# Order of the VectorE and ScalarE work between norm and up projection in a hybrid decoder layer

## The chip, the cores and the metric

The kernel runs on one core of a Trainium2 chip. The metric is the device time of one execution in microseconds; the kernel before took 1312.49 us (median of 3 runs, 1310.65 to 1314.9).

A core has engines that each work through a queue of their own in order: TensorE (PE in the profile) multiplies matrices, VectorE (DVE) does elementwise arithmetic on two operands, ScalarE (ACT) does copies and functions of one operand, GpSimd (POOL) does further elementwise work, and SyncE (SP) issues the DMAs here. [...] An instruction that waits holds up all that stands behind it on its engine.

## The reference, cut to what matters

One decoder layer on `x` of 1024 tokens by 1024 channels: a norm, one input projection whose columns feed differential attention and a gated delta rule, an output projection onto the residual, and a squared-ReLU MLP. The change lies at the start of that MLP.

```python
x = x + mix @ w_out[l]
h = rms_norm(x, norm2_w[l])
x = x + jnp.square(jax.nn.relu(h @ w_up[l])) @ w_down[l]
```

`h` is 1024 x 1024, `w_up` 1024 x 4096 and `w_down` 4096 x 1024, all in float32.

## The kernel before

Three things shape the part around the change.

First, each float32 matrix product is made of three matmuls on rounded operands: an operand is split into a rounded part (ACT: `S.copy`, L1124) and the rest, the operand minus its rounded part (DVE, L1125); the rest-by-rest product is left out. `split` does both, ACT first and then DVE.

Second, the up projection takes seven block products where plain 2 x 2 blocking takes eight (Strassen's way in Winograd's order). For that, sums and differences of blocks are made. On the side of `h` they are made once, for four tiles of 128 tokens (tb 0 to 3, the second block of tokens): `s1`, `s2` are the transposed halves of the tile's normed rows, `t1` and `t4` its differences to the tile four further on, kept in `kept`. The results are the operands hH/hL (rounded part and rest of `h`) and T_ops: T0 for product 6, T1 for product 7, T2 for product 4. On the side of `w_up` they are made for each of the eight groups g of 512 columns: four raw blocks a, b, c, d, of which `combine` makes the operands of the products 5, 6, 3 and 7 in place (`WS`, L1283: 5 is c = c + d, 6 is c = c - a, 3 is b = b - c, 7 is c = d - c), each of which is then split. An `op` tile is a rounded part or a rest; there are five.

Third, PE's order is written out by hand throughout. A product is 24 matmuls of 128 x 512. For group 0 the products 1 and 2 (into banks X0 and Y) run before the seam, as do those of group 1 (X1 and Z); then come, for group 0, product 5 (into Y, after `read_first` has read it), 6 (onto X0), 3 (onto Y), 7 (onto X0), then product 5 of group 1 (into Y afresh), and product 4 of group 0. Before a product is added onto a bank, the bank's value so far has to be copied out: Y to `d` by ACT (L1373), X to `c` by ACT (L1375), Y's sum into `c` by DVE (L1377).

The *seam* runs from L1264 to L1426. In it the order of DVE and of ACT is by hand too (`manual_schedule` over PE, DVE and ACT): the instructions of the seam stay in the order in which the program gives them, though work from before and behind it can be put between them. Outside the seam a planner orders DVE, ACT and the DMAs, by a model of the times of its own.

The steps that the seam orders are, for the four tiles, the stages of `held_back` (L1154), called by `held(stage, tiles)`: stage 0 is `second` (s1 from s2 and s1, L1150; split of the second half into hH/hL, L1151; s2 minus t1, L1152), stage 1 the split of T0, stage 2 the difference `t4` (L1154), stage 3 the split of T1, stage 4 the split of T2. For the operands they are `rounded(g, i)` (the combination, then ACT's rounding, L1326) and `rest(g, i)` (DVE's rest, L1330). `read_first` (L1239) copies X0 on ACT, adds Y on DVE, applies ReLU and square on ACT and stores the result. `step(g, i)` emits a product and what reads its bank. `load_w` (L1287) loads raw blocks for the coming groups, each into a buffer that must have come free.

The part of the seam that is not inside a function:

```python
held(0, [0, 1]); held(1, [0, 1]); rounded(0, 5); held(0, [2]); read_first(); rest(0, 5)
held(0, [3]); held(1, [2, 3]); rounded(0, 6); rest(0, 6)
...
rounded(0, 3); rest(0, 3); step(0, 5); held(3); held(2, [0, 1]); held(4, [0, 1])
rounded(0, 7); rest(0, 7); step(0, 6); held(2, [2, 3]); held(4, [2, 3])
for g, i in ((1, 1), (1, 2), (0, 3)): step(g, i)
```

(Printed with several calls on a line; in the program each has its own, L1336 to L1345 and L1413 to L1425.)

Of the kernel before, what the change touches and what calls it, by code (L numbers as in the profile page):

```python
# [9 lines left out]
F32 = mybir.dt.float32  # L10
# [3 lines left out]
ALU = mybir.AluOpType  # L14
# [90 lines left out]
def act(n, accum=False):  # L105
    return "S", 55.0 + 0.83 * n + (93.0 if accum else 0.0)


def vec(n, extra=0.0):
    return "V", 68.0 + 1.045 * n + extra  # L110
# [7 lines left out]
def tile_hymba_layer(  # L118
# [7 lines left out]
    V, S, G, T = nc.vector, nc.scalar, nc.gpsimd, nc.tensor  # L126
# [26 lines left out]
    hH = hpool.tile([P, KB, SEQ], F32R, name="hH")  # L153
    hL = hpool.tile([P, KB, SEQ], F32R, name="hL")
# [236 lines left out]
    def ta(name, bufs, dt=F32):  # L391
        return sa.tile([P, 512], dt, tag=name, name=name, bufs=bufs)
# [93 lines left out]
    for h, hf, y, th in skew(dn_proj(1)):  # L486
        k2 = ta("k2", 2)
# [5 lines left out]
        for c in range(4):  # L493
            i = cidx(h, 4 * hf + c)
# [9 lines left out]
        for c in range(4):  # L504
            i = cidx(h, 4 * hf + c)
# [56 lines left out]
    for h, hf, y, th in skew(dn_proj(0)):  # L562
        k2 = ta("kr", 2)
# [7 lines left out]
        for c in range(4):  # L571
            i = cidx(h, 4 * hf + c)
# [3 lines left out]
        for c in range(4):  # L576
            i = cidx(h, 4 * hf + c)
# [541 lines left out]
    normed_by, normed_at, held_back, banks, normed2, raws, kept, u, ups = [], {}, [], {}, set(), [], {}, {}, {}  # L1119
    k1, k2, tok1, tok2 = slice(0, 4), slice(4, 8), slice(512, 1024), slice(0, 512)  # L1120

    def split(dst, src):

        S.copy(dst[0], src)  # L1124
        V.tensor_tensor(dst[1], src, dst[0].bitcast(F32), ALU.subtract)  # L1125
# [5 lines left out]
    def turn_b(hn, t, tb):  # L1131
        sl = slice(tb * P, (tb + 1) * P)
        for i in range(2):
            r = yield from flow.bank("px", at=t)
            p = px.tile([P, 512], F32, tag="px", name="ps_tr")
            for j in range(4):
                T.transpose(p[:, j * P:(j + 1) * P], hn[i][:, j * P:(j + 1) * P], ident)
            S.copy(hn[i], p)
            flow.pe(4 * TR)
            t = flow.chain(act(512))  # L1140
            flow.hold(r, t)
        s1, s2 = [x.rearrange("p (k c) -> p k c", k=4) for x in hn]
        t1, t4 = kept[tb + 4][:, 0], kept[tb + 4][:, 1]
        T2, T3, T4 = [[x[:, :, sl] for x in o] for o in T_ops]
        V.tensor_tensor(t1, s1, t1, ALU.subtract)
        split((hH[:, k1, sl], hL[:, k1, sl]), t1)
        flow.chain(vec(512), act(512), vec(512), start=t)

        def second():
            V.tensor_tensor(s1, s2, s1, ALU.subtract)  # L1150
            split((hH[:, k2, sl], hL[:, k2, sl]), s2)  # L1151
            V.tensor_tensor(s2, s2, t1, ALU.subtract)  # L1152

        held_back.append((second, lambda: split(T2, s2), lambda: V.tensor_tensor(t4, t4, s2, ALU.subtract),  # L1154
                          lambda: split(T3, s1), lambda: split(T4, t4)))

    def backs():
        while len(normed_at) < NT:
            d = next((d for d in sorted(hns) if hns[d][1] <= flow.now), None)
            if d is None or not state["free"]:  # L1160
                yield flow.now + 50, None
                continue
            hn, t = hns.pop(d)
            if d < 4:
                keep(tiles[d])
                for i in range(2):
                    yield from turn(hn[i], t, tiles[d], 4 * i, kept[tiles[d]][:, i])
                feed()
                normed_at[d] = landed[tiles[d], 4]
            else:  # L1170
                yield from turn_b(hn, t, tiles[d])
                normed_at[d] = flow.now
# [66 lines left out]
    def read_first():  # L1239
        a0 = pools["uz"].tile([P, 2, 512], F32, tag="ua0", name="ua0")  # L1240
        S.copy(a0, banks["X0"])
        V.tensor_tensor(a0, a0, banks["Y"], ALU.add)
        act2(a0)
        nc.sync.dma_start(ud[1][0], a0)
        u[0] = {"a": a0}
# [66 lines left out]
    def flush(keep):  # L1312
        while len(puts) > keep:
            for d, t in puts.pop(0):
                nc.sync.dma_start(d, t)
# [3 lines left out]
    def combine(g, i):  # L1319
        dst, l, r, op = WS[i]  # L1320
        V.tensor_tensor(w[g][dst], w[g][l], w[g][r], op)

    def rounded(g, i):
        combine(g, i)
        early[g, i] = [op_.tile([P, 4, 256], F32R, tag="op", name="op", bufs=5) for _ in range(2)]
        S.copy(early[g, i][0], w[g][CH[i]])  # L1326

    def rest(g, i):
        o = early[g, i]
        V.tensor_tensor(o[1], w[g][CH[i]], o[0].bitcast(F32), ALU.subtract)  # L1330

    def held(stage, tbs=range(4)):
        for i in tbs:
            held_back[i][stage]()

    held(0, [0, 1])  # L1336
    held(1, [0, 1])
    rounded(0, 5)
    held(0, [2])
    read_first()  # L1340
    rest(0, 5)
    held(0, [3])
    held(1, [2, 3])
    rounded(0, 6)
    rest(0, 6)  # L1345

    def product(g, i):
        if i in WS and (g, i) not in early:
# [59 lines left out]
    def step(g, i):  # L1408
        puts.append([])
        product(g, i)  # L1410
        flush(2)

    rounded(0, 3)  # L1413
    rest(0, 3)
    step(0, 5)
    held(3)
    held(2, [0, 1])
    held(4, [0, 1])
    rounded(0, 7)
    rest(0, 7)  # L1420
    step(0, 6)
    held(2, [2, 3])
    held(4, [2, 3])
    for g, i in ((1, 1), (1, 2), (0, 3)):
        step(g, i)  # L1425
    seam.close()  # L1426
# [146 lines left out]
```

## Time and profile before

| | |
|---|---|
| median of 3 runs | 1312.49 us (1310.65 to 1314.9) |
| the profiled execution | 1312.03 us, its span 1310.2 us |
| PE busy | 1246.2 us (95% of the span) |
| DVE busy | 879.2 us (67%) |
| ACT busy | 599.3 us (46%) |
| POOL busy | 269.7 us (21%) |
| mean granted clock of TensorE | 0.986 |

The span is the time from the first to the last instruction of the profiled execution; 1.8 us of its time lie around it. Rows of a timeline give start, length, engine, source line, operation, the tile written and the tiles read, shapes, and how many like instructions are merged; in brackets stands the idle time of the engine before the row and what ended it. Lengths of neighbours on an engine overlap a little, so the time that a piece of work takes is the distance from its start to the next start. Where a helper makes an instruction, the row shows the helper's line: L1124 and L1125 are `split`, L1321 is `combine`.

### The profile page before, as it was taken

What the parts mean: (1) busy time and instruction counts of PE and PEld (TensorE: products, weight loads), DVE (VectorE), ACT (ScalarE), POOL (GpSimd) and SP (SyncE); (2) the same over time, 40 slices, a digit from 0 to 9 for tenths busy, and PEclk for the clock granted to TensorE, in tenths of its full rate; (3) what the DMA queues carried; (4) which work ended last, traced back from release to release, by engine and by line L of the source; (5) the groups of instructions that cost most, each with busy time, mean ns of one, the idle gap of its engine ahead of it and who ended that gap; (6) DMA issues with size and microseconds to landing.
All of it is one profiled execution on the core that took longest, in us unless ns stands there. A gap on an engine that the chain in (4) does not pass through costs nothing.

```text
span 1310.2 us, 18982 instructions
## 1 busy us (share of the span) xinstructions
PE 1246.2 (95%) x6925; PEld 1067.6 (81%) x6925; DVE 879.2 (67%) x1413; ACT 599.3 (46%) x1171; POOL 269.7 (21%) x320
## 2 busy tenths in 40 slices
PE   6998888999999899999999999999999999999998
PEld 6987666789898899788878788888887788888887
DVE  6469999856764876667478855555666775577552
ACT  5254433334343666555475645444554433333331
POOL 1048866124543542111220000000000000000000
PEclk9999889999998999999999999999999999999999
DMA  7144344436765464623343744334347955523311
GB/s 248 41 113 111 108 108 108 106 102 213 235 211 177 159 187 154 194 71 111 108 162 104 264 147 150 135 142 151 145 176 247 403 188 193 193 95 99 127 64 65
DMA packets 164775, 200.30 MB, mean 153 GB/s; under 512 B 20249, under 2 KB 125001, under 8 KB 164681
## 3 DMA queue, kind: packets, MB, share of 16 engines
q1 hardware_dynamic: 164680, 199.07, 46.4%
q8 instruction: 55, 0.90, 0.3%
q14 instruction: 40, 0.32, 0.1%
HBM read 132.97 MB, written 66.06 MB: 152 GB/s over the span
## 4 chain that ended last, share of the span: by engine, by line
PE 74%; DVE 14%; DMA 6%; issue 2%; ACT 2%; POOL 1%; SPq 1%; DVEq 0%; POOLq 0%; ACTq 0%
PE X L1202 4%; PE X L1203 4%; PE X L1204 4%; PE X L1495 4%; PE X L1494 4%; PE X L1496 4%; DVE cy L413 3%; PE ps_qk L790 3%; PE ps_qk L791 3%; PE ps_qk L792 3%; PE Y L1202 2%; PE Y L1203 2%; PE Y L1204 2%; PE ps_o L951 2%; PE ps_op L1038 2%
## 5 line engine op out<-in xcount | busy, mean ns | idle before, releaser
L1124 ACT CAST hH<-ur 128x1024 fp32r<-128x1024 f32 x56 | 58.6, 1050 | 175.1 <-PE Z L1495 83.7
L1125 DVE TENSOR_TENSOR hL<-ur,hH 128x1024 fp32r<-128x1024 f32 x56 | 68.3, 1222 | 83.5 <-ACT hH L1124 83.5
L790 PE MATMUL ps_qk<-wH,hH 128*128 128x256 f32 x384 | 114.9, 299 | 0.0
L791 PE MATMUL ps_qk<-wL,hH 128*128 128x256 f32 x384 | 109.0, 284 | 0.0
L792 PE MATMUL ps_qk<-wH,hL 128*128 128x256 f32 x384 | 109.0, 284 | 0.0
L1125 DVE TENSOR_TENSOR op<-raw,op 128x1024 fp32r<-128x1024 f32 x48 | 58.7, 1223 | 73.4 <-PE X L1203 38.7
L1495 PE MATMUL X<-hL,hH 128*128 128x512 f32 x224 | 87.3, 390 | 2.1 <-DVE hL L1125 2.1
L1494 PE MATMUL X<-hH 128*128 128x512 f32 x224 | 87.3, 390 | 1.6 <-DVE b L1393 1.6
L172 POOL TENSOR_TENSOR wL<-wraw,wH 128x512 fp32r<-128x512 f32 x56 | 72.8, 1311 | 70.5 <-ACT wH L171 70.2
L1496 PE MATMUL X<-hH,hL 128*128 128x512 f32 x224 | 87.2, 389 | 0.0
L177 PE MATMUL ps_dn<-hH,wH 128*128 128x512 f32 x192 | 77.8, 405 | 1.0 <-ACT cp L409 1.0
L178 PE MATMUL ps_dn<-hL,wH 128*128 128x512 f32 x192 | 77.9, 405 | 0.0
L179 PE MATMUL ps_dn<-hH,wL 128*128 128x512 f32 x192 | 77.1, 402 | 0.0
L790 PEld LDWEIGHTS ps_qk<-wH,hH 128*128 128x128 f32 x384 | 74.0, 193 | 0.1
L791 PEld LDWEIGHTS ps_qk<-wL,hH 128*128 128x128 f32 x384 | 73.6, 192 | 0.1
L792 PEld LDWEIGHTS ps_qk<-wH,hL 128*128 128x128 f32 x384 | 73.1, 190 | 0.0
L413 DVE SCALAR_TENSOR_TENSOR cy<-cp,pv,cy 128x512 f32<-128x512 f32 x72 | 65.7, 917 | 9.5 <-ACT cy L411 8.1
L1125 DVE TENSOR_TENSOR hL<-dw,hH 128x1024 fp32r<-128x1024 f32 x56 | 68.0, 1217 | 4.4 <-ACT hH L1124 4.4
L1124 ACT CAST op<-raw 128x1024 fp32r<-128x1024 f32 x48 | 50.4, 1052 | 34.5 <-PE Y L1204 19.9
L171 ACT CAST wH<-wraw 128x512 fp32r<-128x512 f32 (+1 forms) x72 | 42.9, 620 | 48.2 <-DMA wraw<-in_w_in_dram 36.4
L1124 ACT CAST hH<-dw 128x1024 fp32r<-128x1024 f32 x56 | 58.4, 1047 | 13.7 <-PE Z L1496 7.4
L912 ACT ACTIVATE pexp<-ps_sc,mx 128x128 f32<-128x128 f32 (+7 forms) x64 | 47.4, 742 | 26.6 <-DVE mx L908 26.1
(337 smaller groups left out, 3608.5 us busy)
## 6 DMA issues: line engine op xcount, KB each, us to landing
ur<-ud SPq DMA_DIRECT2D x28, 1024.0 KB, 4.9
raw<-in_w_up_dram SPq DMA_DIRECT2D x32, 512.0 KB, 3.9
dw<-in_w_down_dram SPq DMA_DIRECT2D x32, 512.0 KB, 7.0
wraw<-in_w_in_dram SPq DMA_DIRECT2D x48, 256.0 KB, 3.2
qk_d<-qa SPq DMA_DIRECT2D x32, 256.0 KB, 2.6
ud<-ua SPq DMA_DIRECT2D x16, 512.0 KB, 3.2
ud<-s SPq DMA_DIRECT2D x16, 512.0 KB, 2.6
pka<-park_d SPq DMA_DIRECT2D x32, 192.0 KB, 3.6
```

The costliest lines, as they stand in the source:

```text
L413: V.scalar_tensor_tensor(y, cp[:, wi + b:wi + b + 512], pv[:, 12 * wi + u:12 * wi + u + 1], y, ALU.mult, ALU.add)
L790: T.matmul(ps[:, :256], hH[:, k, sl], wh[:, k, :], start=(k == 0), stop=False)
L791: T.matmul(ps[:, :256], hH[:, k, sl], wl[:, k, :], start=False, stop=False)
L792: T.matmul(ps[:, :256], hL[:, k, sl], wh[:, k, :], start=False, stop=(k == KB - 1))
L1124: S.copy(dst[0], src)
L1125: V.tensor_tensor(dst[1], src, dst[0].bitcast(F32), ALU.subtract)
L1202: T.matmul(ps, op[0][:, k, cs], h[0][:, k, :], start=start and k == 0, stop=False, skip_group_check=True)
L1203: T.matmul(ps, op[0][:, k, cs], h[1][:, k, :], start=False, stop=False, skip_group_check=True)
L1204: T.matmul(ps, op[1][:, k, cs], h[0][:, k, :], start=False, stop=stop and k == 3, skip_group_check=True)
L1494: T.matmul(bank[t], v[0][:, j, sl], v[2][:, j], start=s0, stop=False, skip_group_check=True)
L1495: T.matmul(bank[t], v[0][:, j, sl], v[3][:, j], start=False, stop=False, skip_group_check=True)
L1496: T.matmul(bank[t], v[1][:, j, sl], v[2][:, j], start=False, stop=s1, skip_group_check=True)
```

## The change

`second` becomes two stages, so that the rounding on ACT and the rest on DVE are queued apart: `first` (L1150, and ACT's half of the split) and `second` (DVE's half of it, and L1152). The stages count 0 to 5 now: 0 `first`, 1 `second`, 2 the split of T0, 3 the difference `t4`, 4 the split of T1, 5 the split of T2. `rounded` no longer makes the combination; `combine` is called by itself, and for the operands 3 and 7 it is called earlier, in the first part of the seam. The differences `t4` come in that part too. `read_first` comes after both stages of the tiles 2 and 3. The rests of the operands 3 and 7 come after the products 5 and 6. Nothing is computed that was not, and nothing is left out.

```diff
@@ -1146,12 +1146,15 @@
         split((hH[:, k1, sl], hL[:, k1, sl]), t1)
         flow.chain(vec(512), act(512), vec(512), start=t)
 
+        def first():
+            V.tensor_tensor(s1, s2, s1, ALU.subtract)
+            S.copy(hH[:, k2, sl], s2)
+
         def second():
-            V.tensor_tensor(s1, s2, s1, ALU.subtract)
-            split((hH[:, k2, sl], hL[:, k2, sl]), s2)
+            V.tensor_tensor(hL[:, k2, sl], s2, hH[:, k2, sl].bitcast(F32), ALU.subtract)
             V.tensor_tensor(s2, s2, t1, ALU.subtract)
 
-        held_back.append((second, lambda: split(T2, s2), lambda: V.tensor_tensor(t4, t4, s2, ALU.subtract),
+        held_back.append((first, second, lambda: split(T2, s2), lambda: V.tensor_tensor(t4, t4, s2, ALU.subtract),
                           lambda: split(T3, s1), lambda: split(T4, t4)))
@@ -1321,7 +1324,6 @@
     def rounded(g, i):
-        combine(g, i)
         early[g, i] = [op_.tile([P, 4, 256], F32R, tag="op", name="op", bufs=5) for _ in range(2)]
         S.copy(early[g, i][0], w[g][CH[i]])
@@ -1335,14 +1337,21 @@
     held(0, [0, 1])
     held(1, [0, 1])
+    held(2, [0, 1])
+    combine(0, 5)
     rounded(0, 5)
-    held(0, [2])
+    held(0, [2, 3])
+    held(1, [2])
+    rest(0, 5)
+    held(1, [3])
     read_first()
-    rest(0, 5)
-    held(0, [3])
-    held(1, [2, 3])
+    combine(0, 6)
     rounded(0, 6)
+    combine(0, 3)
+    held(2, [2, 3])
     rest(0, 6)
+    combine(0, 7)
+    held(3)
@@ -1411,16 +1420,13 @@
     rounded(0, 3)
+    step(0, 5)
     rest(0, 3)
-    step(0, 5)
-    held(3)
-    held(2, [0, 1])
-    held(4, [0, 1])
+    held(4)
     rounded(0, 7)
+    step(0, 6)
     rest(0, 7)
-    step(0, 6)
-    held(2, [2, 3])
-    held(4, [2, 3])
+    held(5)
     for g, i in ((1, 1), (1, 2), (0, 3)):
         step(g, i)
```

In the code T2, T3 and T4 (L1144) are the names of one tile's slices of T0, T1 and T2 in the profile. `first` and the rest of `held_back` are called through `held`, the operands' steps directly.

## The prediction

> **What bounds the kernel now.** I read first the page, for the span and the engine that carries the chain; then the view of waits for TensorE (PE) in the second half of the span; then the table by stretches around the longest of those waits; then the timelines of PE, VectorE (DVE), ScalarE (ACT) and SyncE's queue (SPq) there. The page's two lines:
>
> ```profile
> span 1310.2 us, 18982 instructions
> PE 74%; DVE 14%; DMA 6%; issue 2%; ACT 2%; POOL 1%; SPq 1%; DVEq 0%; POOLq 0%; ACTq 0%
> ```
>
> PE carries the end, so only time in which PE stands or runs slowly can be won. Lines of PE's waits after 500 us (total, times, longest):
>
> ```profile
> PE X L1202 <- ACT c L1375: 2.4, 1, 2.4
> PE X L1495 <- DVE hL L1125: 2.1, 1, 2.1
> PE X L1494 <- DVE b L1393: 1.6, 1, 1.6
> ```
>
> The first is at the seam that the change rewrites; the others stand at the start of the down projection. The stretches (us, then busy time with counts for PE, PEld, DVE, ACT, POOL; granted clock; DMA share; GB/s):
>
> ```profile
> 725.40:728.00 2.60, 0.27 (x2) 0.00 (x0) 1.49 (x2) 1.98 (x3) 0.00 (x0) 1.00 0.96 301
> 729.50:733.00 3.50, 3.50 (x10) 2.73 (x9) 3.50 (x6) 2.32 (x4) 0.00 (x0) 0.51 0.62 170
> 736.00:980.00 244.00, 244.00 (x1078) 202.12 (x1077) 143.79 (x128) 124.22 (x123) 0.00 (x0) 1.00 0.44 160
> ```
>
> PE stands, runs at a clock of 0.51 for 3.5 us, and is full from 736 to 980 with DVE at 144 of 244 us: whatever the seam wins is not lost to a second bound in the up loop. PE's timeline (start, length, line, tile):
>
> ```profile
> 709.07 0.40 PE L1202 MATMUL Y<-hH,op 128*128 128x512 f32 x1
> 714.55 0.39 PE L1202 MATMUL X<-T0h,op 128*128 128x512 f32 x1
> 720.07 0.39 PE L1202 MATMUL Y<-hH,op 128*128 128x512 f32 x1
> 725.28 0.39 PE L1204 MATMUL Y<-hH,op 128*128 128x512 f32 x1
> 728.03 0.50 PE L1202 MATMUL X<-T1h,op 128*128 128x512 f32 x1 [2.36 <-ACT c L1375]
> 729.52 0.62 PE L1202 MATMUL X<-T1h,op 128*128 128x512 f32 x1
> 732.93 0.40 PE L1204 MATMUL X<-T1h,op 128*128 128x512 f32 x1
> 735.02 0.39 PE L1204 MATMUL X<-T1h,op 128*128 128x512 f32 x1
> 735.47 0.47 PE L1202 MATMUL Y<-hH,op 128*128 128x512 f32 x1
> ```
>
> Products of 24 matmuls begin at 709.07 (5), 714.55 (6), 720.07 (3), 728.03 (7) and 735.47 (the next group's 5). From 714.55 to 720.07 one takes 5.52 us, 0.23 a matmul. Product 7 could have begun at 725.28 + 0.23 = 725.51 and ended at 731.03; its successor begins at 735.47. **The seam loses 4.44 us**: 2.52 for the late start, 0.1 in the restart, 1.57 in the slow clock (8 matmuls in the 3.41 us from 729.52 to 732.93, which need 1.84), and 0.22 in the last gap.
>
> Why it is late stands on DVE and ACT:
>
> ```profile
> 718.56 2.50 DVE L1125 TENSOR_TENSOR T1l<-hn,T1h 128x512 fp32r<-128x512 f32 x4 [0.21 <-ACT T1h L1124]
> ...
> 722.42 1.23 DVE L1321 TENSOR_TENSOR raw<-raw 128x1024 f32<-128x1024 f32 x1 [0.16 <-DMA raw<-in_w_up_dram]
> ...
> 724.77 1.22 DVE L1321 TENSOR_TENSOR raw<-raw 128x1024 f32<-128x1024 f32 x1
> 734.11 1.21 DVE L1377 TENSOR_TENSOR c<-c,Y 128x1024 f32<-128x1024 f32 x1
> ```
>
> ```profile
> 717.91 2.18 ACT L1124 CAST T1h<-hn 128x512 fp32r<-128x512 f32 x4
> 726.02 1.04 ACT L1326 CAST op<-raw 128x1024 fp32r<-128x1024 f32 x1 [3.10 <-DVE raw L1321]
> 726.97 1.01 ACT L1375 COPY c<-X 128x1024 f32<-128x1024 f32 x1
> ```
>
> Product 7 adds onto the bank that ACT must first copy to `c` (L1375). That copy's input is ready at about 720.3, when product 6 ends, but it is queued behind the rounding of operand 7 (L1326), and this waits for the combination of operand 7, DVE's row at 724.77, which stands behind four T1 rests, two L1154, a combination of the next group (722.42) and two T2 rests. The last gap has its cause in the 734.11 row: Y's sum into `c` ends at 735.32, and only then may the next product overwrite Y.
>
> **The change part by part.** It adds and removes no arithmetic and no DMA: the same instructions stand in other places of DVE's and ACT's queues. So the cost is what is late at each product. Unit prices: 1024-wide on DVE 1.14 (713.66 to 714.80, below); 512-wide 0.61 (the 718.56 row: 2.50 less the 0.68 of one, over 3); ACT 1024-wide 0.95 (726.02 to 726.97), 512-wide 0.55 (717.91 row over 4).
>
> ```profile
> 701.49 0.68 DVE L1150 TENSOR_TENSOR hn<-hn 128x512 f32<-128x512 f32 x1
> 703.26 0.69 DVE L1125 TENSOR_TENSOR hL<-hn,hH 128x512 fp32r<-128x512 f32 x1 [1.09 <-ACT hH L1124]
> 704.66 1.21 DVE L1242 TENSOR_TENSOR ua<-ua,Y 128x1024 f32<-128x1024 f32 x1
> 708.61 0.69 DVE L1125 TENSOR_TENSOR hL<-hn,hH 128x512 fp32r<-128x512 f32 x1 [0.99 <-ACT hH L1124]
> 713.66 1.22 DVE L1330 TENSOR_TENSOR op<-raw,op 128x1024 fp32r<-128x1024 f32 x1 [1.12 <-ACT op L1326]
> 714.80 1.22 DVE L1321 TENSOR_TENSOR raw<-raw 128x1024 f32<-128x1024 f32 x1
> ```
>
> ```profile
> 705.91 1.06 ACT L1248 ACTIVATE ua<-ua 128x1024 f32<-128x1024 f32 x1 [1.77 <-DVE ua L1242]
> 707.00 1.06 ACT L1249 ACTIVATE ua<-ua 128x1024 f32<-128x1024 f32 x1
> ```
>
> Up to the first tile step at 701.49, DVE does the same set of work (tiles 0 and 1, combination 5), so I let the new order start there. **First and second split**: tiles 2 and 3 both subtract (701.49, 702.10) while ACT rounds; the first rest still starts at 703.26, but the second no longer has the idle 0.99 of the 708.61 row. Then: square term 703.87, rest 5 at 704.48, tile 3 at 705.62 and 706.23.
>
> **read_first later**: its sum from Y moves from 704.66 to 706.84 and ends at 708.05. Product 5 writes Y at 709.07: 1.0 us left. ACT's two passes, queued behind that sum, run 708.05 to 710.1 (lengths 1.09 from 705.91 to 707.00, and 0.95), and everything queued behind them on ACT waits: rounding 6, T0 of tiles 2 and 3, rounding 3, ending at 713.1. Its store to DRAM goes some 2 us later on SPq; the loads queued behind it there start with the buffer that combination 6 frees, at 709.1, so they lose nothing against today's 712.5.
>
> **Combinations 6, 3 and 7 alone**: DVE does 6 and 3 from 707.98 to 710.3, stands until ACT's T0 (1.4 us, which costs nothing as PE has product 5), then T0's rests 711.6 to 712.9, rest 6 to 714.07 (today 714.88; product 6 wants it at 714.55 plus two matmuls), combination 7 to 715.2, four L1154 to 717.6, rest 3 to 718.8 (wanted at 720.5). Hidden under products 5 and 6; uncovered, a slip over 0.8 us is PE's one for one.
>
> **Operand 7**: its combination is done at 715.2, not 726.0. ACT copies Y, does four T1 (to 718), rounds 7 (to 719), and the copy to `c` runs when product 6 ends: 720.3 to 721.3, against 725.5 needed. DVE has T1's rests by 721.2, rest 7 by 722.4, T2 by 724.8. The 2.36 us wait goes, with its restart. **Next in line** is Y's sum into `c`: two 512-wide sums, then 726.0 to 727.2, wanted at 731.03; two or three pieces of the next group may be put ahead of it as today (1.14 each), which leaves at least 0.4. A load of raw weights behind rest 3 is also a step that is passed:
>
> ```profile
> 718.38 0.37 SPq L1294 DMA_DIRECT2D raw<-in_w_up_dram  x1
> ```
>
> ```profile
> raw<-in_w_up_dram SPq DMA_DIRECT2D x32, 512.0 KB, 3.9
> ```
>
> Today it goes out at 718.38, just behind rest 3; then at 718.8, and it lands 3.9 later, at 722.7. A combination that waited for it ahead of rest 7 would make rest 7 end at 725.0: still in time. Between a leftover of 0 and the 1.0 us that one more piece on DVE would cost I take 0.
>
> **The slow clock** is not in the code. This trace has stalls of like length with and without it:
>
> ```profile
> 205.27 0.66 PE L442 MATMUL ps_t<-ident,k 128*128 128x128 f32 x4 [2.47 <-DVE k L566]
> 369.82 1.16 PE L652 MATMUL ps_A<-sr,W 128*128 128x128 f32 x8 [2.20 <-DVE sr L644]
> ```
>
> ```profile
> 204.00:208.00 4.00, 2.73 (x18) 1.00 0.46 131
> 370.00:374.00 4.00, 4.00 (x25) 0.64 0.65 205
> ```
>
> After 2.47 us of standing the clock stays at 1.00, after 2.20 it falls to 0.64. So the 1.57 belongs to this stall here, but need not be in every execution: its worth lies between 0 and 1.57, and I take the whole, as in the trace. [...]
>
> **Sum.** 4.44 us off the profiled execution's 1312.03 us (span 1310.2 plus 1.8 around it) is 1307.6. That run stands 0.46 under the median 1312.49, which the forecast is for: 1312.49 - 4.44, about **1308.0 us**.
>
> **The rivals.** *Smaller win (A):* the slow stretch stays or is missing in the timed executions, or about a microsecond is left at Y's sum or at product 5. For it: the mixed rows of the clock, and the 0.8 to 1.0 us margins. Against: the clock is 1.00 from 736 to 980 without stalls. 4.44 - 1.57 = 2.9, so 1309.6 us.
>
> [...]
>
> *Slower (C):* DVE and ACT are ordered by hand only up to the end of the seam; behind it the planner lays their order from its own clock, which the change moves. If it puts combinations that wait for a load ahead of Y's sum (L1377), PE waits there in every group. Y's sum is done some 1.4 us after the product and wanted 5.5 after it, a cover of 4.1. Two combinations (2.3) and one landing (3.9) ahead of it exceed that by 2.1 us; in all six groups that is 12.6, so 1320.6 us; slower than before from three groups on. For it: a combination was put into the middle of the seam at 722.42. Against: PE has no wait in 244 us now, and loads begin no later.
>
> *It does not do what it says (D):* the planner puts other ACT work ahead of the copy to `c`, and the wait stays: 1312.5. Against: the slack there is 4.2 us.
>
> **Chances.** Forecast 0.66 (own range 1306 to 1309.2), A 0.10, B and D together 0.08, C 0.16. About 0.3%, or 3.9 us, is what a measurement can tell from no change: faster means under 1308.6, slower over 1316.4. The forecast lies 0.6 us inside, so 0.08 of its 0.66 falls to the same; A and 0.06 of B and D are the same; C is slower, and so are 0.02 of B and D with more drops than two. Faster 0.58, same 0.24, slower 0.18. The range is 1305.8 (the two later stalls, 3.7 us together, shrink by some 2) to 1314.0, which leaves out C.
>
> **What would show it.** In the new profile: no PE wait on L1375, product 7 beginning at about 725.5 and the next at 731.0, clock 1.00 from 725 to 736; combination 7 on DVE before 716; idle of the kind in the 708.61 row gone; Y's first write still at 709.1. Wrong: a PE wait at 709 to 715 on DVE or ACT (margins eaten), waits on L1377 in later groups (C), or clock drops near 998 and 1045 (B).

## The result, and the profile after

The changed kernel takes 0.9967 of the time of the kernel before (95% interval 0.9952 to 0.9981; 19 runs each), about 4.3 us less, with an interval from 2.5 to 6.3 us. The medians, 1305.87 and 1308.95 us, lie 3.1 us apart, which is inside that interval too. A second measurement, beside some of the experiments, gave 0.9964 (0.9952 to 0.9976). The forecast was 4.44 us less, or 0.34%: the difference and its direction came as forecast. The time itself was forecast at 1308.0 us, with an own range of 1306 to 1309.2, and came 2.1 us lower, 0.1 us below that range. The base of the sum, the median 1312.49 us of three runs, lay 3.5 us over the median of the nineteen; that the medians differ by 3.1 us and not by 4.44 takes 1.4 us of this back.

The profiled execution took 1306.42 us. The page's two lines, then PE's waits after 500 us (total, times, longest), then the stretches (us, busy time with counts for PE, PEld, DVE, ACT, POOL; granted clock; DMA share; GB/s):

```profile
span 1304.7 us, 18985 instructions
PE 74%; DVE 15%; DMA 5%; issue 3%; ACT 2%; POOL 1%; SPq 0%; DVEq 0%; ACTq 0%; POOLq 0%
```

```profile
PE X L1501 <- DVE hL L1125: 2.1, 1, 2.1
PE ps_at L939 <- DVE hL L216: 1.8, 1, 1.8
PE X L1500 <- DVE b L1402: 1.4, 1, 1.4
```

```profile
725.40:728.00 2.60, 2.60 (x13) 2.14 (x12) 2.60 (x5) 2.15 (x3) 0.00 (x0) 1.00 1.07 353
728.00:736.00 8.00, 8.00 (x37) 6.63 (x36) 6.89 (x8) 6.33 (x8) 0.00 (x0) 1.00 0.94 290
736.00:980.00 244.00, 244.00 (x1078) 202.13 (x1077) 141.07 (x126) 120.73 (x119) 0.00 (x0) 1.00 0.45 162
```

The wait for the copy to `c` is gone, PE is full from 725.4 to 980, and its clock stays at 1.00. Rows of the timeline (lines have moved: L1324 is `combine`, L1328 ACT's rounding, L1384 the copy of X to `c`, L1386 Y's sum into `c`):

```profile
702.66 0.69 DVE L1154 TENSOR_TENSOR hL<-hn,hH 128x512 fp32r<-128x512 f32 x1 [0.49 <-ACT hH L1151]
708.47 0.40 PE L1205 MATMUL Y<-hH,op 128*128 128x512 f32 x1
711.42 1.29 DVE L1125 TENSOR_TENSOR T0l<-hn,T0h 128x512 fp32r<-128x512 f32 x2 [1.28 <-ACT T0h L1124]
713.88 1.23 DVE L1324 TENSOR_TENSOR raw<-raw 128x1024 f32<-128x1024 f32 x1
713.95 0.39 PE L1205 MATMUL X<-T0h,op 128*128 128x512 f32 x1
717.14 1.05 ACT L1328 CAST op<-raw 128x1024 fp32r<-128x1024 f32 x1
719.39 0.39 PE L1205 MATMUL Y<-hH,op 128*128 128x512 f32 x1
719.59 1.02 ACT L1384 COPY c<-X 128x1024 f32<-128x1024 f32 x1 [1.40 <-PE X L1207]
723.32 1.22 DVE L1324 TENSOR_TENSOR raw<-raw 128x1024 f32<-128x1024 f32 x1
724.83 0.39 PE L1205 MATMUL X<-T1h,op 128*128 128x512 f32 x1
726.85 1.21 DVE L1386 TENSOR_TENSOR c<-c,Y 128x1024 f32<-128x1024 f32 x1
730.27 0.39 PE L1205 MATMUL Y<-hH,op 128*128 128x512 f32 x1
735.71 0.39 PE L1205 MATMUL X<-T2h,op 128*128 128x512 f32 x1
```

The products now follow one another at 5.44 to 5.48 us: 5 at 708.47, 6 at 713.95, 3 at 719.39, 7 at 724.83, the next group's 5 at 730.27, and 4 at 735.71. From product 5 to product 4 PE takes 27.24 us. In the profile before, product 4 starts at 741.00:

```profile
741.00 0.39 PE L1202 MATMUL X<-T2h,op 128*128 128x512 f32 x1
```

There this stretch is 741.00 - 709.07 = 31.93. So 4.69 us of the 5.5 us between the two spans were won here, and 0.60 lie ahead of product 5, where both kernels do the same.

Three distances are enough to follow the rest: where product 5 of group 0 starts, how long after it DVE starts Y's sum into `c`, and how long after it product 4 starts. All from the timelines, in us:

| kernel | product 5 starts | Y's sum, after it | product 4, after it | ratio to before |
|---|---|---|---|---|
| before | 709.07 | 25.04 | 31.93 | |
| before, second profile | 703.99 | 24.81 | 31.70 | |
| before, third profile | 703.39 | 24.79 | 31.69 | |
| changed | 708.47 | 18.38 | 27.24 | 0.9967 (0.9952 to 0.9981) |
| changed, second profile | 705.19 | 18.38 | 27.23 | 0.9964 (0.9952 to 0.9976) |
| combination 7 early, alone | 704.20 | 23.32 | 30.20 | 1.0000 (0.9983 to 1.0017) |
| changed, combination 7 late | 704.40 | 18.69 | 27.24 | 0.9960 (0.9947 to 0.9973) |
| halves of the split apart, alone | 704.80 | 25.80 | 32.69 | 1.0012 (0.9998 to 1.0026) |
| copy to `c` first | 705.29 | 24.80 | 31.69 | 1.0021 (1.0005 to 1.0037) |
| operand steps, alone | 703.92 | 19.16 | 27.69 | 0.9969 (0.9957 to 0.9982) |
| changed, 3 more on DVE | 704.05 | 20.19 | 27.73 | |
| changed, 8 more on DVE | 705.73 | 27.74 | 37.24 | |
| changed, Z first | 705.25 | 18.38 | 27.24 | 0.9976 (0.9963 to 0.9989) |
| changed, Z first and halves late | 705.25 | 18.38 | 27.24 | 0.9980 (0.9969 to 0.9991) |

### The profile page after: what moved, and what is told of

The parts are those of the page before. It is cut to its first block, busy times and chain, and to the rows that moved or that the text cites. A ratio compares the mean times of both kernels' runs of the same rounds, so it can differ in the third digit from the quotient of the medians.

```text
span 1304.7 us, 18985 instructions
## 1 busy us (share of the span) xinstructions
PE 1246.3 (96%) x6925; PEld 1068.3 (82%) x6925; DVE 879.0 (67%) x1413; ACT 599.4 (46%) x1171; POOL 269.7 (21%) x320
## 4 chain that ended last, share of the span: by engine, by line
PE 74%; DVE 15%; DMA 5%; issue 3%; ACT 2%; POOL 1%; SPq 0%; DVEq 0%; ACTq 0%; POOLq 0%
PE X L1205 4%; PE X L1206 4%; PE X L1207 4%; PE X L1501 4%; PE X L1500 4%; PE X L1502 4%; DVE cy L413 3%; PE Y L1206 2%; PE Y L1205 2%; PE Y L1207 2%; PE ps_qk L790 2%; PE ps_qk L791 2%; PE ps_o L951 2%; PE ps_qk L792 2%; PE ps_op L1038 2%
## 5 line engine op out<-in xcount | busy, mean ns | idle before, releaser
L413 DVE SCALAR_TENSOR_TENSOR cy<-cp,pv,cy 128x512 f32<-128x512 f32 x72 | 63.0, 879 | 9.4 <-ACT cy L411 8.1
```

The costliest lines, as they stand in the source:

```text
L413: V.scalar_tensor_tensor(y, cp[:, wi + b:wi + b + 512], pv[:, 12 * wi + u:12 * wi + u + 1], y, ALU.mult, ALU.add)
```

## The experiments

### One step alone: combination 7 early

```diff
     def rounded(g, i):
-        combine(g, i)
+        if i != 7:
+            combine(g, i)
...
     step(0, 5)
+    combine(0, 7)
     held(3)
```

> The kernel before with one step moved: the combination of operand 7 goes ahead of T1's split, everything else as it was. Theory (the time is set by when ACT reaches the copy of X to c, and that by when DVE makes combination 7): combination 7 is done at about 720, ACT's rounding 7 comes behind two roundings of T2 at about 723 to 724, the copy to c ends at about 725; PE's wait on L1375 goes, at most 0.5 us is left on rest 7, the clock stays at 1.00 there, and the time is 3.5 to 4.4 us under the kernel before (ratio 0.9966 to 0.9973). Rival (it is the alternation of DVE and ACT over two tiles that brings the gain): the wait of PE stays at 1.5 us or more and the time is within 1.5 us of the kernel before.

The ratio was 1.0000 (0.9983 to 1.0017). The wait on the copy to `c` is gone, as the theory had it, but the gain of 3.5 to 4.4 us did not come:

```profile
719.76 1.00 ACT L1376 COPY c<-X 128x1024 f32<-128x1024 f32 x1
725.19 1.22 DVE L1321 TENSOR_TENSOR raw<-raw 128x1024 f32<-128x1024 f32 x1
726.33 1.28 DVE L1370 TENSOR_TENSOR ua<-ua,Z 128x512 f32<-128x512 f32 x2
727.52 1.21 DVE L1378 TENSOR_TENSOR c<-c,Y 128x1024 f32<-128x1024 f32 x1
728.88 0.47 PE L1202 MATMUL Y<-hH,op 128*128 128x512 f32 x1 [1.79 <-DVE c L1378]
```

The copy ends at 720.76, and product 7 starts at 720.82, less than 0.2 us late. One product later PE stands 1.79 us, because Y's sum into `c` starts only at 727.52; a combination of the next group (725.19) stands ahead of it. The stretch to product 4 is only 1.5 us shorter than in the second and third profile of the kernel before (below), which is inside the interval of the times. The theory that went into this run failed: when ACT reaches the copy does not set the time alone. Y's sum in the kernel before was late as well, and that had been hidden behind the wait for the copy.

### One step put back: combination 7 late in the changed kernel

```diff
-    combine(0, 7)
     held(3)
...
+    combine(0, 7)
     rounded(0, 7)
```

> The changed kernel with one step put back: combination 7 directly ahead of its rounding, as in the kernel before. Theory (what counts is what stands ahead of combination 7 on DVE, and t4 and T2 no longer do): combination 7 is done at about 722, the copy to c at about 724.3 on the clock of the changed kernel, PE wants it at 724.8; no wait of PE over 0.3 us, time as the changed kernel within 0.5 us. Rival (the early place of combination 7 is what brings the gain): PE waits 1.5 us or more at product 7, and 2 to 4.4 us of the gain are lost.

0.9960 (0.9947 to 0.9973), no wait, 27.24 us. So the early place of this combination is not what brings the gain. With `t4` and T2 no longer ahead of it, the late place still lets the copy to `c` end at 718.86, 1.9 us before product 7 starts (720.76).

### Only the halves of the split apart

```diff
+        def first():
+            V.tensor_tensor(s1, s2, s1, ALU.subtract)
+            S.copy(hH[:, k2, sl], s2)
         def second():
...
     held(1, [0, 1])
+    held(2, [0, 1])
     rounded(0, 5)
-    held(0, [2])
-    read_first()
+    held(0, [2, 3])
+    held(1, [2])
     rest(0, 5)
-    held(0, [3])
-    held(1, [2, 3])
+    held(1, [3])
+    read_first()
+    held(2, [2, 3])
     rounded(0, 6)
```

(The later stages only get their new numbers.)

> The kernel before with only the two halves of the second split queued apart, so that DVE and ACT alternate over two tiles; the combinations, t4 and T2 stay where they were. Theory: DVE saves about 1.5 us of idle time (1.09 and 0.99 become 0.5 and 0); it carries to combination 7 as far as no other wait takes it, so PE's wait at product 7 falls from 2.4 to between 0.9 and 2.4 us, and the time is 0 to 3 us under the kernel before. Rival (the alternation is the gain): PE's wait goes and the time is 4 us under.

1.0012 (0.9998 to 1.0026): no gain. Two waits of PE in this kernel's timeline:

```profile
711.63 0.50 PE L1207 MATMUL X<-T0h,op 128*128 128x512 f32 x1 [0.53 <-DVE op L1333]
724.51 0.50 PE L1205 MATMUL X<-T1h,op 128*128 128x512 f32 x1 [2.16 <-ACT c L1380]
```

The 2.16 us is inside what the theory allowed, but rest 6 is late too, by 0.53, and Y's sum starts 25.80 us behind product 5, 0.8 to 1.0 us later than in the kernel before. DVE still waits 1.11 us each for the roundings of 3 and 7, as in the kernel before. And what it saves at the second split (the waits of 1.09 and 0.99 us became one of 0.49) it loses at T0, whose roundings stand on ACT behind the two passes of `read_first`, which come later here:

```profile
706.80 1.29 DVE L1125 TENSOR_TENSOR T0l<-hn,T0h 128x512 fp32r<-128x512 f32 x2 [2.72 <-ACT T0h L1124]
```

In the changed kernel the combinations 6 and 3 stand ahead of that row, and the wait is 1.28.

### The copy to c first

```diff
     held(4, [0, 1])
-    rounded(0, 7)
-    rest(0, 7)
     step(0, 6)
+    rounded(0, 7)
+    rest(0, 7)
```

> The kernel before with ACT's copy of X to c ahead of rounding 7 instead of behind it. Theory: the copy ends at about 721.3, but operand 7 itself is no earlier, or up to 1 us later: rounding 7 ends at about 727, its rest at 728.3; PE's wait moves to operand 7 (L1326 and L1330) and is 1.5 to 2.5 us; the time is within 1.5 us of the kernel before. Rival (only the order in ACT's queue was wrong): PE's wait goes, the time is 4 us under.

```profile
723.09 0.50 PE L1202 MATMUL X<-T1h,op 128*128 128x512 f32 x1 [1.22 <-ACT op L1326]
724.35 0.50 PE L1204 MATMUL X<-T1h,op 128*128 128x512 f32 x1 [0.53 <-DVE op L1330]
731.45 0.47 PE L1202 MATMUL Y<-hH,op 128*128 128x512 f32 x1 [1.81 <-DVE c L1377]
```

The wait moved to operand 7 (1.22 and 0.53), as expected, and again 1.81 us at Y's sum. The stretch is 31.69 us, as in the second and third profile of the kernel before; the ratio, 1.0021, means 2.7 us more (0.7 to 4.8), over the 1.5 us that the theory allowed, and the seam does not show them. Where they lie stays open.

### The other half of the change alone

```diff
     def rounded(g, i):
-        combine(g, i)
...
+    combine(0, 5)
     rounded(0, 5)
...
     held(0, [3])
-    held(1, [2, 3])
+    combine(0, 6)
     rounded(0, 6)
+    combine(0, 3)
+    held(1, [2, 3])
     rest(0, 6)
+    combine(0, 7)
+    held(2)
```

(Behind it the order of the changed kernel: rest 3, T1's split, rounding 7, product 6, rest 7, T2's split.)

> The kernel before with the other half of the change: combinations alone and early, rests and T steps behind the products as in the changed kernel, but the second split is not queued apart and the tiles do not alternate. From the first four runs the theory is now: DVE's total of idle time in the seam sets how late Y's sum into c is, and PE waits for whichever of the copy to c, operand 7 and Y's sum is last. Theory: the three waits for roundings (1.12, 1.11 and 1.11 us on DVE) go, the two of 1.09 and 0.99 stay; Y's sum is then some 2 us earlier than PE wants it; from product 5's start to product 4's PE needs 27.2 to 27.8 us (before 31.9, changed 27.2), and the time is as the changed kernel within 1 us. Rival (the alternation over two tiles is needed as well): PE waits 1.5 us or more there, and half of the gain or more is missing.

0.9969 (0.9957 to 0.9982): the whole gain, within the interval, without the alternation over two tiles. The stretch is 27.69 us, 0.45 over the changed kernel's, and this is where:

```profile
708.86 1.22 DVE L1329 TENSOR_TENSOR op<-raw,op 128x1024 fp32r<-128x1024 f32 x1
709.63 0.39 PE L1203 MATMUL X<-T0l,op 128*128 128x512 f32 x1
710.13 0.50 PE L1204 MATMUL X<-T0h,op 128*128 128x512 f32 x1
```

Rest 6 ends at 710.08, and the first matmul that reads it starts at 710.13, 0.50 behind its neighbour instead of 0.23. In the changed kernel rest 6 starts at 712.63 and ends 0.10 ahead of product 6 (713.95). So the alternation is worth about half a microsecond, at this one place.

### The kernel before, twice more

> The kernel before, unchanged, for a second profile. [...]

> [...] The start of product 5 (709.07 in the first) shows how much of the spread between executions lies ahead of the seam: more than 2 us if the base moves there, under 1 us if it does not.

The second profile; a stretch, then rows of the timeline:

```profile
722.00:731.00 9.00, 8.18 (x28) 6.31 (x29) 9.00 (x11) 6.47 (x8) 0.00 (x0) 0.81 0.75 236
```

```profile
722.72 0.50 PE L1202 MATMUL X<-T1h,op 128*128 128x512 f32 x1 [2.15 <-ACT c L1375]
728.80 1.21 DVE L1377 TENSOR_TENSOR c<-c,Y 128x1024 f32<-128x1024 f32 x1
730.16 0.47 PE L1202 MATMUL Y<-hH,op 128*128 128x512 f32 x1
```

The third:

```profile
722.00:730.00 8.00, 6.21 (x26) 4.88 (x27) 8.00 (x11) 5.54 (x8) 0.00 (x0) 1.00 0.78 232
```

```profile
722.09 0.50 PE L1202 MATMUL X<-T1h,op 128*128 128x512 f32 x1 [2.13 <-ACT c L1375]
727.44 0.39 PE L1204 MATMUL X<-T1h,op 128*128 128x512 f32 x1
728.18 1.21 DVE L1377 TENSOR_TENSOR c<-c,Y 128x1024 f32<-128x1024 f32 x1
729.53 0.47 PE L1202 MATMUL Y<-hH,op 128*128 128x512 f32 x1 [1.70 <-ACT ua L1248]
```

The same wait at product 7, once with the slow clock (0.81 over the stretch) and once without (1.00). Yet both need the same time, 31.70 and 31.69 us: without the slow clock PE finishes product 7 earlier and then stands 1.70 us. (The row names ACT's L1248, which ends 0.02 us later but does not touch Y; the sum that frees Y, L1377, ends at 729.39.) So the slow clock does come and go, but the stretch is no shorter without it: 31.93 less the 1.57 of the prediction would be 30.4 us, and 31.69 came. In each of the profiles with a late sum PE's next product starts 1.35 to 1.36 us behind the start of Y's sum: 728.80 to 730.16, 728.18 to 729.53, 727.52 to 728.88 (combination 7 alone), 734.11 to 735.47 (the first profile). That sum sets the end of the seam.

The reverse was not tried: no run makes Y's sum early and leaves the copy to `c` late. An estimate from the third profile: the last matmul of product 7 starts at 727.44 and needs 0.23, so PE could have gone on at 727.67 instead of 729.53, and some 1.9 of the 4.5 us would be won. In the first profile, where product 7 ran on the slow clock, it would be 0.2. Neither wait alone is worth the whole.

The start of product 5 moved by 5.7 us between the first and the third profile, with the same program. But only the first profiles of the two kernels are that late: the other twelve in the table lie between 703.39 and 705.73, and the second and third, taken on one chip, are 0.60 apart. The chip of the first pair is not on record, so it stays open whether the 5 us are a matter of the chip or of the execution.

### More on DVE in the changed kernel

```diff
-                          lambda: split(T3, s1), lambda: split(T4, t4)))
+                          lambda: split(T3, s1), lambda: split(T4, t4),
+                          lambda: V.tensor_tensor(T4[1], t4, T4[0].bitcast(F32), ALU.subtract)))
...
     held(5)
+    held(6, [0, 1, 2])
```

That makes three more; for eight more, `held(6)` stands there twice instead, over all four tiles. There is one profile of each and no ratio.

> The changed kernel with three more rests of T2 (repeats of the same instruction with the same result, 0.605 us each on DVE) directly behind T2's split, ahead of Y's sum. Theory (PE's next product starts 1.36 us behind the start of Y's sum, or when product 7 ends, whichever is later): Y's sum starts 18.4 + 1.8 = 20.2 us behind the start of product 5, product 7 ends at 21.8; 20.2 + 1.36 = 21.6, so PE does not wait; from product 5's start to product 4's 27.2 to 27.5 us. Rival (DVE has no such slack, or the copy to c alone counts): 29 us or more, or in the next kernel no change either.

> The changed kernel with eight more rests of T2 at the same place, 4.84 us of DVE. Theory: Y's sum starts 18.4 + 4.8 = 23.2 us behind the start of product 5, up to 1.2 more if the planner puts a piece of the next group ahead of it; PE's next product starts at 24.6 to 25.8 instead of 21.8; from product 5's start to product 4's 30.1 to 31.3 us. The copy to c and operand 7 are as early as in the changed kernel. Rival (the wait at product 7 for the copy to c was the cause, and DVE's lateness at Y's sum does not count): 27.2 to 27.5 us.

With three more, Y's sum starts at 20.19 us as worked out, and PE doesn't wait for it. The stretch is 27.73 us, 0.2 over what was allowed, because the rest of the next operand is now just late:

```profile
726.64 0.50 PE L1208 MATMUL Y<-hH,op 128*128 128x512 f32 x1 [0.18 <-DVE op L1125]
```

With eight more (rows of the timeline, then a stretch):

```profile
724.73 1.22 DVE L1125 TENSOR_TENSOR op<-raw,op 128x1024 fp32r<-128x1024 f32 x1
728.27 1.22 DVE L1325 TENSOR_TENSOR raw<-raw 128x1024 f32<-128x1024 f32 x1
730.54 1.21 DVE L1392 TENSOR_TENSOR ud<-ud,X 128x1024 f32<-128x1024 f32 x1
733.47 1.21 DVE L1387 TENSOR_TENSOR c<-c,Y 128x1024 f32<-128x1024 f32 x1
734.83 0.77 PE L1206 MATMUL Y<-hH,op 128*128 128x512 f32 x1 [7.14 <-DVE c L1387]
```

```profile
728.00:742.00 14.00, 7.17 (x20) 5.78 (x21) 11.75 (x13) 7.17 (x7) 0.00 (x0) 0.63 0.95 323
```

PE stands 7.14 us at Y's sum, although the copy to `c` and operand 7 are as early as ever; it starts 1.36 behind the sum again. The rival falls. The size was missed: the 4.84 us of added work became 27.74 - 18.38 = 9.4, because the planner pulled four pieces of the next steps ahead of the sum, not one (three of them above), and product 4 came at 37.24 instead of at most 31.3, with a slow clock behind the long wait: its matmuls run 0.43 apart there (735.39 to 735.82) instead of 0.23, at the 0.63 of the stretch.

### The start of the down projection

```diff
-    bankA = [X[0][:, 0], X[0][:, 1]] + Z
+    bankA = Z + [X[0][:, 0], X[0][:, 1]]
```

The second kernel also makes each half of a difference of `w_down` blocks just ahead of its own split.

> The changed kernel with the first bank group of the down projection in another order: Z's banks, free early, ahead of X0's, which waits for the last read of b. Theory: PE's wait of 1.4 us on that read falls under 0.3 us, the wait of 2.1 us on DVE at about 1039 stays as it is or grows by what PE came earlier (then the gain is given back there); 0 to 1.4 us under the changed kernel. Rival: the transfers of w_down set that stage's end, and nothing is won at all, the later wait growing to 3.4 us.

> The changed kernel with two edits at the start of the down projection: the first bank group begins with Z's banks, which are free early, and the second half of each difference of w_down blocks is made just ahead of its own split. Theory: PE's wait of 1.4 us for b's read of X0 shrinks to under 0.3, that of 2.1 us on DVE at about 1039 to under 1; nothing else moves; 1.5 to 3.3 us under the changed kernel. Rival (the planner puts the work elsewhere and a wait of the same size comes back on another row, or the transfers set it): within 1 us of the changed kernel.

0.9976 (0.9963 to 0.9989) and 0.9980 (0.9969 to 0.9991), against 0.9964 (0.9952 to 0.9976) for the changed kernel: no better. With Z first the wait of 1.4 us is gone, and the next one is longer by just that:

```profile
1025.67 2.29 DVE L1528 TENSOR_TENSOR dw<-dw 128x2048 f32<-128x2048 f32 x1 [2.25 <-DMA dw<-in_w_down_dram]
1035.88 0.70 PE L1501 MATMUL Z<-hL,hH 128*128 128x512 f32 x1 [3.48 <-DVE hL L1125]
```

3.48 us instead of 2.06, with DVE waiting 2.25 us for a block of `w_down` (1.65 in the first profile of the changed kernel). PE came 1.4 us earlier to a point that the transfers and DVE's work on them set: the rival held, for both kernels (3.7 us in the second).

## Why the prediction was right, and where it was wrong

- **The loss in the seam, 4.44 us: right in sum, wrong in its parts.** It measured 4.69 in the first pair of profiles and 4.5 in the second and third (31.70 and 31.69 against 27.23). Three products at 5.44 instead of 5.52 or 5.53 us account for the difference of the first. The sum asked only that PE be full behind product 5, whichever wait came last; the walk through the new order had put Y's sum in time too. So the size came out although the cause named for it was not the one that set the time.
- **"Why it is late": the step that failed.** The prediction took the wait for the copy to `c` as the cause, and Y's sum as next in line behind it with at least 0.4 us to spare after the change, three pieces of the next group ahead of it. The runs show that in the kernel before Y's sum was already the later of the two; the wait for the copy, the restart and the slow clock lay in its shadow. Taking the wait away alone leaves 30.20 of 31.7 us, so 3.0 of the 4.5 us lost are still there; making Y's sum late alone, with the copy in time, costs 10.0 us (37.24 against 27.24). After the change Y's sum has 2.1 us to spare (726.85 plus 1.36, against 730.27), with one such piece ahead of it. The row that told it was in the prediction: the last gap of 0.22 us, before which Y's sum ends at 735.32. It was read as a small term of its own, and was the end of the chain that set the whole.
- **The slow clock, 1.57 us: not a term.** It comes and goes (0.81 over the stretch in the second profile, 1.00 in the third) and costs nothing there (31.70 and 31.69 us), as Y's sum is late with or without it. With that falls rival A's 1309.6, so far as it rested on the clock.
- **What the change gives DVE: right.** From combination 5 to Y's sum DVE needs 27.10 us (699.75 to 726.85), before 33.76 (700.35 to 734.11). Of the 6.66, 4.0 are idle time: seven waits of 5.79 us in all (five stand in the rows of the prediction, the other two, of 1.11 us each, are at the rests of operands 3 and 7) became two of 1.77, the 0.49 and 1.28 in the rows above. Another 2.3 are two pieces of the next group that the planner no longer puts ahead of the sum (three before, one after, at 723.32; 1.14 each).
- **The walk through the new order: right to some tenths.** Combination 7 was forecast done by 715.2 on the old clock, 6.1 us behind product 5; it ended at 715.1, 6.6 behind it. The copy to `c` was forecast at 11.2 us behind product 5 and started at 11.1; Y's sum at 16.9 and started at 18.4, with one piece ahead of it as allowed.
- **Rivals B, C and D** did not come: at the start of the down projection (B) the waits are 2.1 and 1.4 us, and the clock is 1.00 from 990 to 1296; PE has no wait from 736 to 980 (C), and the copy is in time (D). A clock under 1.00 behind the wait of 2.1 us does come in other profiles, of the kernel before too (last section).
- **The base: wrong.** 1312.49 was a median of three. The start of product 5 in fourteen profiles lies between 703.39 and 709.07, with the same work ahead of it; the profile before had the latest of all, and the profile after the second latest. Why is open, as said above. But on one chip, too, 34 runs of the kernel before, beside the first experiments, lie between 1305.50 and 1312.44 us. A sum of differences was put onto a base that moves by more than the sum.

## What to carry to other kernels

Where several things are late on one engine, the first wait in the trace only shows which comes first: ask for each later reader of the same queue whether it would be in time if the first wait were gone. Here the test was one subtraction, the start of Y's sum plus 1.36 us against the end of the product. And a gain of 4 us should be forecast as a difference, with the spread between executions of the same program (here some 7 us on one chip) looked at before an absolute time is named.

## What had not been expected of the hardware

The same stall of PE, 2.05 to 2.06 us at the start of the down projection, is followed by full or by reduced clock from one execution to the next. Twelve of the profiles have it; six show a granted clock of 0.99 over 990 to 1296 us, in which it lies, the other six 1.00, and the six take some 1.6 us more to the end (from the first matmul of the down projection 313.3 to 313.4 us against 311.8). The kernel before alone shows both: full clock in its first and second profile, reduced in its third. Two of the twelve, each with the stall and the stretch around it (us, PE busy with count, clock, DMA share, GB/s); the changed kernel:

```profile
1039.06 0.50 PE L1501 MATMUL X<-hL,hH 128*128 128x512 f32 x1 [2.06 <-DVE hL L1125]
```

```profile
1030.00:1050.00 20.00, 17.95 (x79) 1.00 0.92 349
```

and the changed kernel with combination 7 late:

```profile
1034.94 0.64 PE L1501 MATMUL X<-hL,hH 128*128 128x512 f32 x1 [2.05 <-DVE hL L1125]
```

```profile
1030.00:1050.00 20.00, 17.95 (x72) 0.91 0.69 261
```

What decides between the two no run here shows.
